# Moving an expert's first transposes and slot rows ahead of the conditional block in a two-layer mixture-of-experts kernel

## The chip, the cores and the metric

One Trainium2 chip; the program uses one core. The metric is the device time of one execution in microseconds (us), as the median of several runs. TensorE's matmul side is called PE below and its weight loads PEld, VectorE is DVE, ScalarE is ACT, GpSimd is POOL, SyncE is SP. A small q behind an engine's name means its instruction sequencer: what the sequencer does by itself (branching, waiting, loading a register) is not counted as busy time of the engine.

## What is computed

A network of three blocks over 256 tokens of width 1024: two layers of attention or convolution, each followed by a mixture of 16 experts, and then one block of a recurrence and a neighbourhood attention. Only the experts matter here:

```python
def hierarchical_moe(hin, w_group, b_group, w_router, b_router, w_gate, w_up, w_down):
    g_prob = softmax(xf @ w_group + b_group)
    g_w, g_idx = top_k(g_prob, 1)                  # one group of four per token
    e_val, e_idx = top_k(e_logits_of_that_group, 2)  # two experts in it
    e_w = softmax(e_val)
    gates = sum(one_hot(g_idx * 4 + e_idx, 16) * (g_w * e_w))
    y = zeros((256, 1024))
    for e in range(16):
        hid = silu(xt @ w_gate[e]) * (xt @ w_up[e])      # 1024 -> 512
        y = y + gates[:, e:e + 1] * (hid @ w_down[e])    # 512 -> 1024
    return y
```

How many tokens choose an expert depends on the data.

## The kernel before

`moe(l, ...)` runs one layer of experts; l is 0 or 1. It ranks the tokens of each expert, and every expert works on a block of 64 slots. If more than 64 tokens chose an expert, further blocks of 64 follow, at most three, each in a nested run-time `If`.

One expert e goes through these steps. `half(e, w, xg, hh)` multiplies the gathered tokens `xg` with the gate and up weights for half hh of the 512 units: `up` writes 32 matmuls into the PSUM tile `gu` (L817, L818), and `hidden` makes `hd` from it with one ACT instruction (`hs`, L828) and one DVE instruction (L829). `turn` transposes `hd` with two PE matmuls into the PSUM tile `hidT` (L836) and copies that to `ht` on DVE (L837). `down` multiplies `ht` with the down weights into `y` (L843). `gated` scales `y` and splits it into two parts `Y` (DVE L850 and L854, ACT L853). `oht_of(e, off)` broadcasts the slot ranks with two small matmuls (`oht` in PSUM, L805) and compares them with the slot numbers on DVE (L807); the result `oht` says which token sits in which slot. `scatter` adds `Y` to the tokens' rows in the four PSUM banks `z` through `oht` (four matmuls, L860).

The loop over e overlaps two experts. At its top stands `more(e, w, nv)`: the `If` over further blocks of expert e (`more_tokens`, in the branch). After it come `turn` for the first half of expert e (whose `hd` was made in the loop's turn before), the load of the next expert's block count `nv` from `xi` (L982, L983), a hint for the next branch, `oht_of`, the second `half` of expert e, `down`, `turn`, `down`, `gated`, then the first `half` of expert e + 1, and at last `scatter` of expert e. So each boundary between two loop turns reads on PE: `z` matmuls, the `If`, `hidT`, `oht`, `gu`.

Every engine meets the `If`. Where it is not entered, an engine jumps to a short block that waits until the engine's own earlier instructions are done and then adds to its semaphore what the skipped instructions would have added ("the bump" below). In the profile it is an EVENT_SEMAPHORE of L920 on the engine's sequencer, and the jump is a COMPARE_BRANCH of L920. An instruction after the `If` that waits for a semaphore value from inside the `If` therefore waits for that engine's bump. Such waits come from shared buffers: the PSUM banks of tags A (`gu`, `gat`) and B (`hidT`, `oht`, `y`, `pq`) have two slots each, and the instructions in the `If` use them too.

PE's order is written out by hand in this loop (`manual_schedule`); DVE and ACT keep the order in which a scheduler puts them. The weights come through a ring of 1 MB buffers that SP fills by DMA as `free(2)` gives them back.

Of the kernel before, what the change touches and what calls it, by code (L numbers as in the profile page):

```python
# [10 lines left out]
F32 = mybir.dt.float32  # L11
F32R = mybir.dt.float32r
# [5 lines left out]
THREE = {mybir.EngineType.PE, mybir.EngineType.DVE, mybir.EngineType.Activation}  # L18
PSUM = bass.MemoryType.PSUM

P = 128
D = 1024
NT = 256
# [149 lines left out]
def model(ctx: ExitStack, tc: tile.TileContext, A, out, stop=None):  # L173
# [472 lines left out]
    def moe(l, wr, lb, pl, late):  # L646
        a2, b2 = mod[f"a2_{l}"], mod[f"b2_{l}"]
        with more_ring, tc.tile_pool(name=f"moe{l}", bufs=1, reuse_waits="tile") as mp, \
# [150 lines left out]
                V.tensor_tensor(gs, pg, par, op=OP.mult)  # L799
                V.tensor_reduce(gc[:, 2 * g:2 * g + 2], gs, axis=AX.X, op=OP.add)  # L800

            def oht_of(e, off):
                p = bank("B", "oht")[:, :256]
                for t in range(2):
                    T.matmul(p[:, t * P:t * P + P], rb[:, t, e:e + 1].to_broadcast([P, P]), identb, start=True, stop=True)  # L805
                o = mw.tile([P, NT], F32R, name="oht")
                V.tensor_scalar(o, p, off, None, op0=OP.is_equal)  # L807
                return o

# [22 lines left out]
            def turn(e, hd, ht, hh):  # L832
                us = slice(64 * (e % 2), 64 * (e % 2) + 64)
                pt = bank("B", "hidT")[:, :128].rearrange("p (c s) -> p c s", c=2)
                for c in range(2):
                    T.transpose(pt[:, c], hd[us, c * P:c * P + P], ident[us, us])  # L836
                V.tensor_copy(ht[:, 2 * hh:2 * hh + 2], pt)  # L837
# [35 lines left out]
            def more_tokens(e, w, b, nv):  # L873
                if b < 3:
                    tc.mark_branch_hint_location(f"more{l}_{e}_{b + 1}", hint=nv > b, engines=[mybir.EngineType.PE])
                us = slice(64 * (e % 2), 64 * (e % 2) + 64)
                oe = mp.tile([P, 2, 2, 64], F32R, name="oe")
                re = mp.tile([P, 2], F32, name="re")
                V.tensor_scalar(re, r[:, :, e], -64.0 * b, None, op0=OP.add)
                for t in range(2):  # L880
                    V.tensor_tensor(oe[:, t], iota64[:, None, :].to_broadcast([P, 2, 64]),
                                    re[:, t:t + 1, None].to_broadcast([P, 2, 64]), op=OP.is_equal)
                off = mp.tile([P, 1], F32, name="off")
                V.tensor_scalar(off, slot, 64.0 * b, None, op0=OP.add)
                xe = mw.tile([P, KD, 64], F32, name="xe", tag="yf", bufs=1)
                for k4 in range(2):
                    pe = bank("A", "gat")
                    for k in range(4 * k4, 4 * k4 + 4):
                        ks, c0 = slice(k * P, k * P + P), P * (k % 4)
                        n = 0  # L890
                        for t in range(2):
                            for src in (th, tl):
                                T.matmul(pe[:, c0:c0 + P], src[:, t, ks], oe[:, t], start=n == 0, stop=n == 3)
                                n += 1
                    for k in range(4 * k4, 4 * k4 + 4):
                        c0 = P * (k % 4)
                        if k % 2:
                            S.activation(xe[:, k], pe[:, c0:c0 + 64], AF.Identity, scale=a2[:, k:k + 1], bias=b2[:, k:k + 1])
                        else:
                            V.tensor_scalar(xe[:, k], pe[:, c0:c0 + 64], a2[:, k:k + 1], b2[:, k:k + 1], op0=OP.mult, op1=OP.add)  # L900
                o = oht_of(e, off)
                pq = bank("B", "pq")[:, :1]
                for t in range(2):
                    T.matmul(pq, oe[:, t].bitcast(F32), gates[:, t, e:e + 1], start=t == 0, stop=t == 1)
                ge1 = mp.tile([P, 1], F32, name="ge1")
                V.tensor_copy(ge1, pq)
                ht = mw.tile([P, 4, 64], F32, name="ht")
                p0 = up(e, w, xe, 0)
                hd0 = hidden(e, p0, ge1[us], "x")
                p1 = up(e, w, xe, 1, lambda: turn(e, hd0, ht, 0))  # L910
                hd1 = hidden(e, p1, ge1[us], "x")
                y = bank("B", "y")
                for cs in halves:
                    down(y, w, ht, 0, cs)
                turn(e, hd1, ht, 1)
                finish(y, w, ht, o)

            def more(e, w, nv):
                def block(b):
                    with tc.If(nv > b - 1, label=f"more{l}_{e}" + (f"_{b}" if b > 1 else "")):  # L920
                        with tc.manual_schedule(engines=THREE):
                            more_tokens(e, w, b, nv)
                        if b < 3:
                            block(b + 1)

                block(1)
# [39 lines left out]
            order.close()  # L966
            Yx = cst.tile([P, 2, 512], F32R, name="Y", tag="x0")
            for e in range(16):
                more(e, w, nv)
                with ExitStack() as part:  # L970
                    if e == 15:
                        if l == 1:
                            fg = x[1]
                            junk2 = mp.tile([P, 512], F32, name="junk2", tag="tl")
                        tail.enter_context(tc.manual_schedule(engines=THREE))
                    else:
                        part.enter_context(tc.manual_schedule(engines={mybir.EngineType.PE}))
                    ht = mw.tile([P, 4, 64], F32, name="ht")
                    turn(e, hd0, ht, 0)
                    if e < 15:  # L980

                        nv = nc.values_load(xi[0:1, e + 1:e + 2], min_val=0, max_val=3)  # L982
                        tc.mark_branch_hint_location(f"more{l}_{e + 1}", hint=nv > 0, engines=[mybir.EngineType.PE])  # L983
                    o = oht_of(e, slot)
                    if e == 15:
                        if l == 1:
                            spread(fg, col("fin"))
                    hd1 = half(e, w, xg, 1)
                    y = bank("B", "y")
                    for cs in halves if e == 15 else (slice(0, 512),):  # L990
                        down(y, w, ht, 0, cs)
                    turn(e, hd1, ht, 1)
                    if e in GA:

                        ks = GA[e]
                        if ks[0] == 0:
                            oh = places(e // 4 + 1)
                            xn = mw.tile([P, KD, 256], F32, name="xg", tag="xg")
                        for k in range(*ks, 2):
                            gather(oh, xn, range(k, k + 2))  # L1000
                    if e == 15:
                        finish(y, w, ht, o)
                        free(2)
                        x[0] = cst.tile([P, D], F32, name="x0")
                        for h in range(2):
                            for t in range(2):
                                cs = slice(h * 512, h * 512 + 512)
                                sq = square(t, h, src=z[t][h])
                                if l == 0:
                                    V.tensor_copy(x[t][:, cs], z[t][h])  # L1010
                                else:

                                    V.tensor_tensor(x[t][:, cs], z[t][h], fg[:, cs], op=OP.mult)
                        if l == 1:
                            for h in range(2):
                                for t in range(2):
                                    cs = slice(h * 512, h * 512 + 512)
                                    if (h, t) in SQD:
                                        V.tensor_tensor_reduce(junk2, x[t][:, cs], x[t][:, cs], 1.0, 0.0, op0=OP.mult, op1=OP.add, accum_out=ssq2[:, t, h:h + 1])
                                    else:  # L1020
                                        sq = square(t, h, ssq2)
                        break
                    down(y, w, ht, 1)
                    free(2)
                    Y = gated(y)[1]
                    w = [take(f"moe{l}", e + 1, t) for t in range(6)]
                    if e % 4 == 3:
                        xg = xn
                        slot_gates(e // 4 + 1, oh)
                    hd0 = half(e + 1, w, xg, 0)  # L1030
                    scatter(o, Y)
# [614 lines left out]
```

## Time and profile before

| what | value |
|---|---|
| median of 3 runs | 1191.7 us (1190.25 to 1200.09) |
| the profiled execution: time, span | 1196.26 us, 1194.4 us |
| PE busy | 1103.3 us, 92% of the span |
| DVE busy | 644.3 us, 54% |
| ACT busy | 415.2 us, 35% |
| granted TensorE clock over the span | 0.983 of full speed |
| experts of layer 0, of layer 1 in the span | about 190 to 425 us, and 594 to 863 us |

The span runs from the first to the last instruction in the trace. Times in rows are from the span's start. In a row of the timeline stand: start, duration, engine, line, operation, output<-inputs, sizes, how many instructions were merged, and in brackets how long the engine had been idle and what released it. In a row of grouped lines the last two parts are the busy time with the mean of one in ns, and the idle time just before these instructions with its releasers.

### The profile page before, as it was taken

How to read it: one execution, taken by the hardware profiler on the slowest of the kernel's cores; microseconds unless marked ns; L12 is line 12 of the kernel's file. 1: busy time of each engine (PE TensorE's matmuls, PEld its weight loads, DVE VectorE, ACT ScalarE, POOL GpSimd, SP SyncE). 2: the span in 40 equal slices, each digit the busy share in tenths (PEclk: the TensorE clock that was granted, in tenths of full speed). 3: DMA queues.
4: the chain of work that ended last, by engine and by line, in shares of the span. 5: the costliest groups of instructions: out<-in, count | busy, mean ns of one | idle time of the engine just before them, and what ended most of it. 6: DMA issues, size and time to landing. Idle time of an engine off the chain costs nothing. (4 is left out here: it accounts for less than half of the span.)

```text
span 1194.4 us, 20819 instructions
## 1 busy us (share of the span) xinstructions
PE 1103.3 (92%) x8172; PEld 787.8 (66%) x8172; DVE 644.3 (54%) x1488; ACT 415.2 (35%) x802; POOL 23.1 (2%) x48
## 2 busy tenths in 40 slices
PE   5899998999999989999998998998889999999996
PEld 3786565555555469867654554554478889788995
DVE  4665564333333359887632333332399897667566
ACT  2434432111111154365311211111257546455443
POOL 0000000000000000000000000000012000000000
PEclk9899989999999999999999999999999999999998
DMA  9999868999999987668857999998466445543440
GB/s 381 406 396 418 333 232 340 416 415 416 418 417 418 396 311 291 241 227 324 343 218 281 406 407 393 381 406 317 170 212 217 156 148 181 177 165 140 146 172 36
DMA packets 51064, 354.42 MB, mean 297 GB/s; under 512 B 6160, under 2 KB 6544, under 8 KB 9296
## 3 DMA queue, kind: packets, MB, share of 16 engines
q1 hardware_dynamic: 48544, 344.59, 73.7%
q0 software_dynamic: 2064, 7.08, 1.9%
q8 instruction: 104, 1.70, 0.6%
q14 instruction: 64, 0.52, 0.1%
q10 hardware_dynamic: 288, 0.52, 0.1%
HBM read 350.07 MB, written 1.05 MB: 294 GB/s over the span
## 5 line engine op out<-in xcount | busy, mean ns | idle before, releaser
L818 PE MATMUL gu<-ring,xg 128*64 128x256 f32 x1024 | 240.6, 389 | 2.3 <-issue 2.3
L817 PE MATMUL gu<-ring,xg 128*64 128x256 f32 x1024 | 240.3, 389 | 1.9 <-issue 1.8
L473 PE MATMUL pw<-xh,wh 128*128 128x256 f32 x736 | 211.5, 289 | 7.5 <-ACT wh L456 2.6
L459 DVE TENSOR_TENSOR wl<-ring,wh 128x1024 fp32r<-128x1024 f32 x144 | 175.2, 1221 | 74.3 <-ACT wh L456 70.2
L475 PE MATMUL pw<-xh,wl 128*128 128x256 f32 x736 | 209.2, 285 | 0.8 <-DVE wl L459 0.8
L474 PE MATMUL pw<-xl,wh 128*128 128x256 f32 x736 | 208.6, 284 | 0.0
L817 PEld LDWEIGHTS gu<-ring,xg 128*64 128x64 f32 x1024 | 139.6, 140 | 70.5 <-issue 11.2
L456 ACT ACTIVATE wh<-ring 128x1024 fp32r<-128x1024 f32 x114 | 120.0, 1058 | 152.4 <-PE pw L474 75.6
L473 PEld LDWEIGHTS pw<-xh,wh 128*128 128x128 f32 x736 | 141.3, 193 | 19.1 <-issue 10.0
L818 PEld LDWEIGHTS gu<-ring,xg 128*64 128x64 f32 x1024 | 139.6, 140 | 18.9 <-issue 10.4
L475 PEld LDWEIGHTS pw<-xh,wl 128*128 128x128 f32 x736 | 141.6, 193 | 3.5 <-DVE wl L459 1.9
L474 PEld LDWEIGHTS pw<-xl,wh 128*128 128x128 f32 x736 | 141.7, 193 | 0.9 <-DVE ge L1084 0.4
L843 PE MATMUL y<-ring,ht 128*64 128x512 f32 (+1 forms) x576 | 128.3, 563 | 6.7 <-DVE ht L837 5.0
L829 DVE SCALAR_TENSOR_TENSOR hd<-hs,gc,gu 64x256 f32<-64x256 f32 x64 | 30.7, 480 | 165.8 <-ACT hs L828 165.8
L828 ACT ACTIVATE hs<-gu 64x256 f32<-64x256 f32 x66 | 25.0, 378 | 252.1 <-PE gu L818 252.1
L353 PE MATMUL ada<-ring,zc 128*32 128x256 f32 x960 | 68.9, 393 | 14.0 <-DMA ring<-ada 11.3
L843 PEld LDWEIGHTS y<-ring,ht 128*64 128x64 f32 x576 | 39.4, 137 | 53.6 <-issue 33.8
L853 ACT ACTIVATE Y<-yf 64x512 fp32r<-64x512 f32 (+1 forms) x72 | 42.7, 593 | 91.3 <-DVE yf L850 90.4
L854 DVE TENSOR_TENSOR Y<-yf,Y 64x512 fp32r<-64x512 f32 (+1 forms) x72 | 46.2, 642 | 22.7 <-ACT Y L853 21.3
L490 PE MATMUL pt<-wh,xh 128*128 128x512 f32 x144 | 57.0, 398 | 1.0 <-ACT wh L456 0.4
L492 PE MATMUL pt<-wl,xh 128*128 128x512 f32 x144 | 56.5, 392 | 0.5 <-DVE wl L459 0.5
L491 PE MATMUL pt<-wh,xl 128*128 128x512 f32 x144 | 56.3, 391 | 0.0
(391 smaller groups left out, 1528.0 us busy)
## 6 DMA issues: line engine op xcount, KB each, us to landing
ring<-moe SPq DMA_DIRECT2D x192, 1024.0 KB, 9.5
ring<-ada SPq DMA_DIRECT2D x60, 1024.0 KB, 9.5
ring<-b_z SPq DMA_DIRECT2D x24, 1024.0 KB, 4.8
ring<-b_x SPq DMA_DIRECT2D x12, 1024.0 KB, 5.5
ring<-od_q SPq DMA_DIRECT2D x8, 1024.0 KB, 10.1
ring<-ev_q SPq DMA_DIRECT2D x6, 1024.0 KB, 18.2
ring<-ev_v SPq DMA_DIRECT2D x4, 1024.0 KB, 15.6
ring<-ev_o SPq DMA_DIRECT2D x4, 1024.0 KB, 15.7
```

Of the source, the lines that this page charges most:

```text
L353: T.matmul(p[32 * j:32 * j + 32, :256], zc[:, k, 7 - r:39 - r], w[:, k], start=start and k < 4, stop=stop and k >= 4, skip_group_check=True)
L456: S.activation(h, w, AF.Copy)
L459: V.tensor_tensor(l, w, h.bitcast(F32), op=OP.subtract)
L473: T.matmul(p, hk, xh[:, k], start=k == 0, stop=False)
L474: T.matmul(p, hk, xl[:, k], start=False, stop=False)
L475: T.matmul(p, lk, xh[:, k], start=False, stop=k == KD - 1)
L490: T.matmul(p[t], xh[:, k, n], hk, start=k == 0, stop=False)
L491: T.matmul(p[t], xl[:, k, n], hk, start=False, stop=False)
L492: T.matmul(p[t], xh[:, k, n], lk, start=False, stop=k == KD - 1)
L817: T.matmul(p[gs_], xg[:, k], wg[:, k], start=k == 0, stop=k == KD - 1)
L818: T.matmul(p[us], xg[:, k], wu[:, k], start=k == 0, stop=k == KD - 1)
L843: T.matmul(y[64 * h:64 * h + 64, cs], ht[:, k], wd[:, k % 2, h, cs], start=k == 0 and cs.start == 0, stop=k == 3, skip_group_check=cs != s ...
```

## The change

`turn(e, hd0, ht, 0)` and `oht_of(e, slot)` now stand ahead of `more(e, w, nv)`, in a block whose order is fixed on PE, DVE and ACT. Inside the `If`, the tiles of the same kind take other memory, so that those made ahead of it stay whole: `ohx` uses the buffer `junk`, and `htx` the buffer `e`.

```diff
-            def oht_of(e, off):
+            def oht_of(e, off, o=None):
                 p = bank("B", "oht")[:, :256]
                 for t in range(2):
                     T.matmul(p[:, t * P:t * P + P], rb[:, t, e:e + 1].to_broadcast([P, P]), identb, start=True, stop=True)
-                o = mw.tile([P, NT], F32R, name="oht")
+                o = mw.tile([P, NT], F32R, name="oht") if o is None else o
                 V.tensor_scalar(o, p, off, None, op0=OP.is_equal)
                 return o
...
-                o = oht_of(e, off)
+                o = oht_of(e, off, wk.tile([P, 512], F32R, name="ohx", tag="junk", bufs=1)[:, :NT])
...
-                ht = mw.tile([P, 4, 64], F32, name="ht")
+                ht = adap.tile([P, 256], F32, name="htx", tag="e").rearrange("p (a b) -> p a b", a=4)
...
             for e in range(16):
+                with tc.manual_schedule(engines=THREE):
+                    ht = mw.tile([P, 4, 64], F32, name="ht")
+                    turn(e, hd0, ht, 0)
+                    o = oht_of(e, slot)
+
                 more(e, w, nv)
...
-                    ht = mw.tile([P, 4, 64], F32, name="ht")
-                    turn(e, hd0, ht, 0)
                     if e < 15:

                         nv = nc.values_load(xi[0:1, e + 1:e + 2], min_val=0, max_val=3)
                         tc.mark_branch_hint_location(f"more{l}_{e + 1}", hint=nv > 0, engines=[mybir.EngineType.PE])
-                    o = oht_of(e, slot)
```

On PE, behind the `If` of expert 1 in layer 0, stood before (the names in brackets are the semaphores that an instruction waits for: DVE_49, PE_49 and Activation_49 count finished instructions of the engines, DMAHW ones landed transfers):

```order
L920 UNCONDITIONAL_BRANCH [waits PE_49] x3
L836 MATMUL hidT<-ident,hd 128x64 [waits DVE_49,PE_49]
L836 MATMUL hidT<-ident,hd 128x64
L982 TENSOR_LOAD xi
L983 REGISTER_ALU
L1634 BRANCH_PREFETCH_HINT
L805 LDWEIGHTS rb [waits DVE_49]
L805 MATMUL oht<-identb,rb 128x128 [waits PE_49]
L805 LDWEIGHTS rb
L805 MATMUL oht<-identb,rb 128x128
L817 MATMUL gu<-ring,xg 64x256 [waits DMAHW3_49,Activation_49]
```

and stands now:

```order
L920 UNCONDITIONAL_BRANCH [waits PE_49] x3
L985 TENSOR_LOAD xi
L986 REGISTER_ALU
L1636 BRANCH_PREFETCH_HINT
L817 MATMUL gu<-ring,xg 64x256 [waits DVE_49,DMAHW3_49,PE_49,Activation_49]
L818 MATMUL gu<-ring,xg 64x256 [waits DMAHW4_49]
```

The wait for DVE_49 has moved from the first `hidT` to the first `gu`. In the built program that `gu` wants a DVE count of 378, while DVE stands at 327 ahead of the `If` and at 387 after its bump; the same holds, with other numbers, behind all 32 of the outermost `If`s (behind the last of layer 1 for the matmuls of L429, which come first there). Ahead of the next `If`, PE now reads:

```order
L860 MATMUL z<-Y,oht 128x512 [waits DVE_49]
L860 MATMUL z<-Y,oht 128x512
L836 MATMUL hidT<-ident,hd 128x64 [waits DVE_49]
L836 MATMUL hidT<-ident,hd 128x64
L805 LDWEIGHTS rb
L805 MATMUL oht<-identb,rb 128x128 [waits PE_49]
L805 LDWEIGHTS rb
L805 MATMUL oht<-identb,rb 128x128
L920 COMPARE_AND_BRANCH
```

Before, the COMPARE_AND_BRANCH stood right behind the `z` matmuls. On DVE, the copy and the comparison now stand ahead of the same `If`, between `hd` and the branch, where before the load of `xi` followed `hd` directly:

```order
L829 SCALAR_TENSOR_TENSOR hd<-hs,gc,gu 64x256 [waits Activation_49]
L837 COPY ht<-hidT 128x128 [waits PE_49]
L807 TENSOR_SCALAR oht<-oht,slot 128x256 [waits PE_49]
L985 TENSOR_LOAD xi
L920 COMPARE_AND_BRANCH
```

DVE's bump waits for both of them. No instruction is added to or taken from PE, DVE, ACT or POOL; on SP one 1 MB transfer of layer 0 stands one `If` earlier.

## Rows read from the trace of the kernel before


**Rows 1.** Windows: busy us and instructions of each engine, PEclk, DMA share, GB/s

```profile
211.00:425.00 214.00, 200.86 (x1436) 113.64 (x1434) 68.69 (x145) 35.41 (x70) 0.00 (x0) 1.00 1.00 410
```

**Rows 2.** Waits of PE: total us, times, longest us

```profile
PE hidT L836 <- DVEq L920: 11.2, 18, 1.8
PE hidT L836 <- PEq L920: 7.5, 14, 1.5
```

**Rows 3.** Lines: busy us, mean ns, then idle ahead and its releasers

```profile
L805 PE MATMUL oht<-identb,rb 128*128 128x128 bf16 x66 | 9.4, 225 | 9.8 <-PE hidT L836 4.9 <-DVE ht L837 4.8
```

**Rows 4.** Timeline at the boundary of expert 1, layer 0

```profile
210.54 1.20 PE L860 MATMUL z<-Y,oht 128*128 128x512 f32 x4
211.13 0.49 DVE L829 SCALAR_TENSOR_TENSOR hd<-hs,gc,gu 64x256 f32<-64x256 f32 x1 [1.07 <-ACT hs L828]
...
212.04 0.31 PE L836 MATMUL hidT<-ident,hd 64*128 64x64 f32 x2 [0.30 <-PEq L920]
...
212.65 0.28 PE L805 MATMUL oht<-identb,rb 128*128 128x128 bf16 x2 [0.31 <-PE hidT L836]
...
212.86 0.43 PE L817 MATMUL gu<-ring,xg 128*64 128x256 f32 x1
...
212.97 0.48 DVE L807 TENSOR_SCALAR oht<-oht,slot 128x256 fp32r<-128x256 f32 x1 [0.30 <-PE oht L805]
```

**Rows 5.** Sequencers there: ns min/median/max, first and last start

```profile
L920 DVEq EVENT_SEMAPHORE  x1: 21/21/21, 211.7 to 211.7; - x1
L920 PEldq EVENT_SEMAPHORE  x1: 51/51/51, 211.8 to 211.8; - x1
```

**Rows 6.** Timeline at the boundary of expert 3, layer 0

```profile
240.67 0.49 DVE L829 SCALAR_TENSOR_TENSOR hd<-hs,gc,gu 64x256 f32<-64x256 f32 x1 [1.07 <-ACT hs L828]
...
241.74 0.31 PE L836 MATMUL hidT<-ident,hd 64*128 64x64 f32 x2 [0.45 <-DVEq L920]
```

**Rows 7.** DVE's sequencer there

```profile
L920 DVEq EVENT_SEMAPHORE  x1: 21/21/21, 241.6 to 241.6; - x1
```

**Rows 8.** Timeline, expert 0, layer 0: transposes with no branch ahead

```profile
202.68 1.89 PE L843 MATMUL y<-ring,ht 128*64 128x512 f32 x8
...
204.50 0.34 PE L836 MATMUL hidT<-ident,hd 64*128 64x64 f32 x2
```

**Rows 9.** Timeline: boundary of expert 15, layer 1, without load and hint

```profile
849.66 0.30 PE L836 MATMUL hidT<-ident,hd 64*128 64x64 f32 x2 [0.30 <-PEq L920]
849.90 0.29 PE L805 MATMUL oht<-identb,rb 128*128 128x128 bf16 x2
850.00 0.29 DVE L837 COPY ht<-hidT 128x128 f32<-128x128 f32 x1 [0.76 <-PE hidT L836]
...
850.33 0.48 DVE L807 TENSOR_SCALAR oht<-oht,slot 128x256 fp32r<-128x256 f32 x1
```

**Rows 10.** Timeline: boundary of expert 0, layer 0

```profile
196.59 0.31 PE L836 MATMUL hidT<-ident,hd 64*128 64x64 f32 x2 [1.84 <-DVEq L920]
...
197.28 0.28 PE L805 MATMUL oht<-identb,rb 128*128 128x128 bf16 x2 [0.38 <-DVE ht L837]
```

**Rows 11.** PE's branch of L920: all, and that of expert 2, layer 0

```profile
L920 PEldq COMPARE_BRANCH  x34: 89/455/3145, 192.1 to 847.7; - x34
...
L920 PEldq COMPARE_BRANCH  x1: 2140/2140/2140, 223.8 to 223.8; - x1
```

**Rows 12.** DMA queue 8 from 223.35 to 223.75: packets, MB, share

```profile
q8 instruction: 1, 0.02, 16.9%
```

**Rows 13.** Timeline at the boundary of expert 9, layer 1

```profile
761.36 0.30 PE L836 MATMUL hidT<-ident,hd 64*128 64x64 f32 x2 [1.55 <-PEq L920]
```

**Rows 14.** Timeline inside expert 7 of layer 1

```profile
729.57 0.43 PE L818 MATMUL gu<-ring,xg 128*64 128x256 f32 x1 [2.26 <-issue]
```

**Rows 15.** Windows around these two, columns as in rows 1

```profile
757.00:765.00 8.00, 6.14 (x50) 3.75 (x48) 2.36 (x5) 0.72 (x2) 0.00 (x0) 1.00 1.00 409
725.00:734.00 9.00, 6.02 (x36) 3.45 (x38) 0.78 (x2) 0.00 (x0) 0.00 (x0) 0.81 1.00 410
```

## Prediction

> **What bounds the kernel now.** I read three views in turn. First the busy time of the engines over the experts of layer 0: PE works for 200.86 of 214 us, DVE for 68.69 and ACT for 35.41, at a granted clock of 1.00 [rows 1]. So PE is the bound there and what can be won or lost is its idle 13 us. DMA's share is 1.00 too, yet among PE's waits none inside the experts names a DMA, so the weights arrive in time, if barely. Next the waits of PE: ahead of `hidT` it idles 11.2 us for DVE's bump (18 times) and 7.5 us for its own (14 times) [rows 2], and ahead of `oht` 9.8 us [rows 3]. Together 28.5 us over the 32 boundaries, nearly all that PE idles in the experts. The two first boundaries of a layer are dearer, 1.84 + 0.38 = 2.22 us [rows 10]; without them (28.5 - 4.4) / 30 = **0.80 us idle at an ordinary boundary**.
>
> Last the timeline of one boundary, with the end of `z` as zero (expert 1: 210.54 + 1.20 = 211.74) [rows 4]. `hd` ended at -0.12. `hidT` starts at +0.30, behind PE's bump (211.8) [rows 5]. `oht` starts only at +0.91, 0.61 behind `hidT`, though in expert 15, which has no load and no hint there, it is 0.24 behind [rows 9, 4]. So the load and the hint hold PE's sequencer about 0.37 us. `gu` starts at +1.12, as `oht` ends. The comparison runs from +1.23 to +1.71: under `gu`, for nothing.
>
> DVE's bump comes in two kinds. In expert 1 it is at 211.7, about 0.1 us after `hd` ended (211.62) [rows 4, 5]. In expert 3 `hd` ended at 241.16 and the bump is at 241.6, 0.44 us later, and `hidT` follows 0.14 us behind it [rows 6, 7]. PE waited for DVE 18 times, two of them at the first boundaries, so 16 of the 30 ordinary ones are of the late kind [rows 2].
>
> **The change, part by part.**
>
> (a) `hidT` and `oht` ahead of the `If`. Nothing is added or removed, so PE's busy time stays. Where no branch stands ahead, `hidT` starts 0.07 us before the modelled end of the matmuls ahead of it (202.68 + 1.89 = 204.57 against 204.50) [rows 8]; `hd` is done by then. So `hidT` at -0.07, `oht` 0.24 later, ended 0.53 after `hidT` started (849.66 to 850.19) [rows 9], which is +0.46. The 0.80 us of idle ahead of these two vanish: -24 us over 30 boundaries, if nothing took their place.
>
> (b) The wait for DVE moves to `gu`. This is what takes its place. `gu` shares its two slots of tag A with the tiles in the `If`, so it waits for a DVE count that only DVE's bump gives. And the bump now stands behind the copy of `ht` and the comparison. In expert 15 the comparison ends 1.15 us after `hidT` starts (849.66 to 850.81) [rows 9], so now at -0.07 + 1.15 = +1.08. The bump follows 0.1 or 0.44 later, PE 0.14 behind it, and two more semaphores at one instruction I price at 0.05 each, what PE's own event took (51 ns) [rows 5]. That gives `gu` at +1.42 (early kind) or +1.76 (late kind).
>
> (c) PE's own way to `gu`. The load and the hint still stand ahead of `gu`, 0.37 us with the instruction behind. Worse, PE's branch was issued before `z` ran and had 1.2 us of `z` as cover; now it is issued behind `oht`, at about +0.2. Its median is 0.455 us [rows 11], so it ends at about +0.65. The jump and the bump behind it were under that cover and have no row on PE; DVE's 0.1 to 0.44 bound them. Then the load, the hint and the waits, some 0.6 us as between `hidT` and `oht`. So PE's own way gives `gu` at +1.4 to +1.7, about the same as DVE's. I take the later of the two: +1.6 in the early kind, +1.76 in the late one.
>
> The mean is (14 x 1.6 + 16 x 1.76) / 30 = +1.69, and PE's idle at a boundary 1.69 - 0.46 = 1.23 us instead of 0.80: **+0.43 x 30 = 13 us**.
>
> (d) The two first boundaries already wait for DVE. There the comparison (0.48 us) [rows 4] comes out from under `gu`: +0.5 each, 1 us. The one boundary that enters the `If` is charged like the others.
>
> (e) What else moves. Behind the waiting `gu` on PE are 32 more matmuls of that half, and behind those ACT's `hs` and DVE's `hd`; they are PE's work or wait for it, so they shift with it. SP's ring transfers are released by PE and shift too; one of layer 0 stands an `If` earlier, and costs nothing, since no boundary waits for a transfer; POOL has no instruction at the boundaries. DVE and ACT are a third busy [rows 1], so the new order costs them nothing but the place of the bump. The buffers `junk` and `e` are touched only in the `If`: 0.
>
> Sum: 13 + 1 = **+14 us**. Against the profiled execution's own 1196.3 us that is 1210; that execution is 4.6 us above the median of the runs, 1191.7, so the median becomes **1206 us**, +1.2%. Its bounds: all boundaries early and PE's way never later than +1.42 gives 30 x (0.96 - 0.80) + 1 = +6 us, 1198; all late gives 30 x (1.30 - 0.80) + 1 = +16, 1208, and 1210 with PE's way 0.07 behind it. So 1198 to 1210 in this case.
>
> **The rivals.**
>
> *PE's branch becomes the bound.* Half of the branches take over 0.455 us, the longest 3.1 us [rows 11]. If that time starts when the branch is issued, the long ones are no longer covered. Take 15 of them at the middle between median and longest, 1.8 us: they end at +2.0 instead of +0.65, and with jump, bump, load and hint (0.75) `gu` starts at +2.75 instead of +1.69. That is 15 x 1.1 = 16 us on top: 1222. Against it: in expert 2 an instruction packet was already moving in the 0.4 us before its 2.14 us branch [rows 12, 11]; if the fetch runs on its own time, a later branch finds it further on and is shorter. The Trainium skill ("Runtime: NRT & Kernel Launch", section Instruction fetch mechanics) says that a taken branch to a target outside the two pages held forces a fetch of that page before execution goes on, which fits branches of 0.09 to 3.1 us and would make the whole of a long one count here; the packet in the row speaks for a fetch that begins earlier.
>
> *PE's own way alone decides, and it is short.* If DVE's bump did not hold `gu` and the branches were short, PE's bump would come 0.1 us after `oht`, and `gu` 0.75 later, at about +1.31: idle 0.85, 30 x 0.05 + 1 = +2.5. Time 1194, no change. Against it stands the count that `gu` wants, which no instruction ahead of the `If` reaches.
>
> *A gain.* If the load, the hint and the bumps all ran while `hidT` and `oht` still worked, PE would only pay the 0.30 us behind its own bump, as expert 15 does now [rows 9], and a little for the waits, 0.5 in all: 30 x (0.50 - 0.80) = -9, 1183. It decides if `gu` starts sooner than +1.26 (0.46 + 0.80). Against it: the comparison alone ends at +1.08, and the load stands behind the bump.
>
> *The clock.* Longer idle could drop it: after an idle time of 2.26 us in expert 7 [rows 14] the stretch of 9 us around it has a mean of 0.81, so part of it ran at 1.2 GHz; after one of 1.55 us [rows 13] the stretch of 8 us kept 1.00, 2.4 GHz [rows 15]. My 1.23 us is on the safe side of both, so I charge nothing; with the long branches of the first rival some would not be.
>
> **How the numbers follow.** My forecast, 1198 to 1210: 0.60. The branch as bound, 1210 to 1222: 0.18. PE's way short, 1192 to 1198: 0.16. The gain: 0.06. A measurement can tell about 1% here, 11.9 us, so slower means above 1203.6. Within my case, two thirds lie above that (0.40), and all of the branch case: slower 0.58. The rest of my case (0.20), the short way and most of the gain lie within 1%: 0.40. Faster by over 1% needs a gain of 12 us, 0.02. The range takes my case, most of the short way and two thirds of the branch case: 1196 to 1218.
>
> **What would show it.** In the profile after: the idle ahead of `hidT` and `oht` gone (28.5 us before); a new idle ahead of `gu` of L817, about 1.2 us at each boundary, some 37 us in all, ended by DVE's bump where the bump is of the late kind; DVE's copy and comparison ahead of its bump, the comparison ending at about +1.1; and the branches on PE, whose median and longest tell the first rival. I am wrong if `gu` starts before +1.26 (then it is no loss), or if the idle ahead of `gu` is ended by PE's bump at over 2 us (then it is the branch).

## The result and the profile after

The changed kernel takes 1216.05 us (median of 4 runs, 1210.12 to 1218.64) against 1193.38 us before (median of 4). The medians lie 22.7 us apart; the ratio is 1.0163, with an interval of 1.013 to 1.0197, which is 19 us. It is slower, by 19 us where I had 14; the range of 1196 to 1218 holds it. A second measurement of the same kernel (below) gave 1.0139 (1.0108 to 1.0169), 17 us. The profiled execution has a span of 1216.7 us against 1194.4.

PE's waits in the profile of after (us in total, times, longest), to be read against [rows 2, 3]:

```profile
PE gu L817 <- DVEq L920: 34.5, 29, 1.5
...
PE gu L817 <- issue: 4.2, 3, 2.6
...
PE gu L818 <- issue: 2.9, 1, 2.9
...
PE gu L817 <- PEq L920: 2.4, 1, 2.4
...
PE row L429 <- DVEq L920: 1.1, 1, 1.1
PE gat L893 <- DVE oe L881: 1.1, 1, 1.1
...
PE hidT L836 <- DVE hd L829: 1.0, 2, 0.5
```

The 28.5 us ahead of `hidT` and `oht` are down to 1.0. In their place stands one new wait: `gu` waits for DVE's bump at 29 boundaries, 34.5 us in all, 1.19 us each.

The boundary of expert 1 in layer 0 of after (timeline, then the sequencers there), against [rows 4, 5]:

```profile
209.82 1.19 PE L860 MATMUL z<-Y,oht 128*128 128x512 f32 x4
...
210.41 0.49 DVE L829 SCALAR_TENSOR_TENSOR hd<-hs,gc,gu 64x256 f32<-64x256 f32 x1 [1.07 <-ACT hs L828]
210.95 0.33 PE L836 MATMUL hidT<-ident,hd 64*128 64x64 f32 x2
211.22 0.28 PE L805 MATMUL oht<-identb,rb 128*128 128x128 bf16 x2
211.32 0.29 DVE L837 COPY ht<-hidT 128x128 f32<-128x128 f32 x1 [0.43 <-PE hidT L836]
...
211.65 0.48 DVE L807 TENSOR_SCALAR oht<-oht,slot 128x256 fp32r<-128x256 f32 x1
212.51 0.40 PE L817 MATMUL gu<-ring,xg 128*64 128x256 f32 x1 [1.01 <-DVEq L920]
```

```profile
L920 PEldq COMPARE_BRANCH  x1: 440/440/440, 211.0 to 211.0; - x1
L920 PEldq EVENT_SEMAPHORE  x1: 51/51/51, 211.5 to 211.5; - x1
L920 DVEq COMPARE_BRANCH  x1: 56/56/56, 212.0 to 212.0; - x1
L920 DVEq EVENT_SEMAPHORE  x1: 21/21/21, 212.2 to 212.2; - x1
```

`z` ends at 211.01. `hidT` starts at -0.06, `oht` ends at +0.49, the comparison ends at +1.12, DVE's bump comes at about +1.2 and `gu` at +1.50. PE's own bump was there at +0.5. PE's branch was issued at about 0.0 (211.0), where I had +0.2. In the boundary of expert 3 the same steps stand, but DVE's bump is of the late kind and `gu` starts at 1.71 behind the end of `z` (240.97):

```profile
242.68 0.40 PE L817 MATMUL gu<-ring,xg 128*64 128x256 f32 x1 [1.22 <-DVEq L920]
```

Where the 22.3 us of the two spans lie, from the waits above, [rows 2, 3] and the page's first part: boundaries 34.5 + 2.4 + 1.0 - 28.5 = 9.4 us; ahead of L429, behind the last `If`, 1.1; ahead of `gat` in the one `If` that is entered 0.6 (0.46 before); gaps inside `gu` that no wait explains 7.1 - 4.1 = 3.0; and PE's busy time 1111.4 - 1103.3 = 8.1, with the same work. Together 22.2. Of the 3.0 us of gaps, 1.3 stand ahead of the first `gu` behind the entered `If`, which the view puts under issue though it is a boundary too.

```profile
PE 1111.4 (91%) x8172; PEld 809.0 (66%) x8172; DVE 643.7 (53%) x1488; ACT 416.5 (34%) x802; POOL 24.0 (2%) x48
```

The busy time grows because TensorE ran longer at its lower clock, 1.2 GHz. Most of that inside the experts lies in one place, the entered `If` of layer 1. There `gat` had to wait for `oe`, which DVE now makes behind the copy and the comparison: 1.09 us of idle instead of 0.46 (after, then before).

```profile
620.67 0.48 DVE L807 TENSOR_SCALAR oht<-oht,slot 128x256 fp32r<-128x256 f32 x1
...
621.28 0.49 DVE L881 TENSOR_TENSOR oe<-iota,re 128x128 fp32r<-128x128 f32 x2
621.62 0.33 PE L893 MATMUL gat<-oe,th 128*128 128x128 f32 x1 [1.09 <-DVE oe L881]
```

```profile
614.22 0.33 PE L893 MATMUL gat<-oe,th 128*128 128x128 f32 x1 [0.46 <-DVE oe L881]
```

These are the windows behind it (from, to, length in us, busy us and instructions of each engine, PEclk, DMA share, GB/s), after first, then before, both some 2.5 us behind the start of `gat`:

```profile
624.00:632.00 8.00, 8.00 (x40) 6.27 (x41) 1.66 (x6) 1.63 (x4) 0.00 (x0) 0.50 0.01 2
```

```profile
617.00:625.00 8.00, 8.00 (x76) 5.65 (x76) 2.26 (x7) 1.69 (x5) 0.00 (x0) 1.00 0.01 4
```

PE is busy throughout in both, but does 40 instructions where before did 76, at a clock of 0.50 instead of 1.00. In all, some 10 us ran at the lower clock there, which costs about 5. An idle time of that length does not do it everywhere: in layer 0 of after `gu` waits 1.0 to 1.3 us at each of these boundaries, and the clock stays at 1.00.

```profile
211.00:425.00 214.00, 194.32 (x1389) 117.42 (x1390) 66.88 (x141) 35.08 (x68) 0.00 (x0) 1.00 0.99 402
```

### The profile page after: what moved, and what is told of

Same layout as the page of the kernel before. It is cut to its first block, busy times and chain, and to the rows that moved or that the text cites. A ratio compares the mean times of both kernels' runs of the same rounds, so it can differ in the third digit from the quotient of the medians.

```text
span 1216.7 us, 20756 instructions
## 1 busy us (share of the span) xinstructions
PE 1111.4 (91%) x8172; PEld 809.0 (66%) x8172; DVE 643.7 (53%) x1488; ACT 416.5 (34%) x802; POOL 24.0 (2%) x48
## 5 line engine op out<-in xcount | busy, mean ns | idle before, releaser
L817 PE MATMUL gu<-ring,xg 128*64 128x256 f32 x1024 | 239.0, 387 | 41.1 <-DVEq L920 34.5
L473 PEld LDWEIGHTS pw<-xh,wh 128*128 128x128 f32 x736 | 141.6, 193 | 19.1 <-issue 10.8
L843 PE MATMUL y<-ring,ht 128*64 128x512 f32 (+1 forms) x544 | 124.9, 575 | 6.4 <-DVE ht L837 4.6
```

The costliest lines, as they stand in the source:

```text
L473: T.matmul(p, hk, xh[:, k], start=k == 0, stop=False)
L817: T.matmul(p[gs_], xg[:, k], wg[:, k], start=k == 0, stop=k == KD - 1)
L843: T.matmul(y[64 * h:64 * h + 64, cs], ht[:, k], wd[:, k % 2, h, cs], start=k == 0 and cs.start == 0, stop=k == 3, skip_group_check=cs != s ...
```

## The experiments

All were timed in five rounds beside the kernel before. The table takes, from each profile: the idle of PE at the boundaries (ahead of `hidT`, `oht` and `gu`, for a bump or for each other; in e1 also the 15.0 us ahead of `gu`), the gaps ahead of `gu` that the view calls issue, and PE's busy time. The ratio is to the kernel before, with its interval.

| kernel | boundaries | gaps in gu | PE busy | ratio |
|---|---|---|---|---|
| before | 28.5 | 4.1 | 1103.3 | 1 |
| after | 37.9 | 7.1 | 1111.4 | 1.0163 (1.013 to 1.0197) |
| a1_after_again | 37.7 | 7.0 | 1105.9 | 1.0139 (1.0108 to 1.0169) |
| e1_only_oht | 50.5 | 0.8 | 1108.1 | 1.0201 (1.0162 to 1.024) |
| e2_only_turn | 42.3 | 4.7 | 1113.8 | 1.0204 (1.0167 to 1.0242) |
| e3_bank_b | 31.4 | 11.0 | 1106.9 | 1.0174 (1.0146 to 1.0203) |
| e4_bank_b_load | 27.6 | 11.1 | 1114.6 | 1.0179 (1.0157 to 1.0201) |
| e5_before_load | 19.1 | 6.0 | 1103.5 | 0.9938 (0.9912 to 0.9965) |
| e6_after_load | 31.3 | 5.6 | 1105.3 | 1.0057 (1.0029 to 1.0085) |
| e7_before_marks | 31.7 | 11.4 | 1112.7 | 1.0109 (1.0067 to 1.0151) |
| e8_bank_b_load_pad | 54.5 | 8.4 | 1125.0 | 1.0434 (1.0395 to 1.0474) |
| e9_load_early | 19.5 | 4.6 | 1101.0 | 0.9913 (0.988 to 0.9946) |

### The changed kernel again (a1_after_again)

> The changed kernel once more, beside before. My sum of the boundaries is +14 us (ratio 1.012); the profile of after shows 22 us more, with fetch gaps inside gu and longer stretches at 1.2 GHz that the sum does not hold. Theory A (bump is all that the change costs, the rest is chance of this execution): ratio 1.010 to 1.014, and the gaps inside gu and the slow stretches lie elsewhere than in the first profile of after. Rival C (the rest belongs to the change too): ratio 1.016 to 1.019, and the slow stretches again behind the entered If and inside layer 1. In both, gu of L817 waits for DVE's bump at 29 boundaries, 33 to 36 us in all.

The ratio, 1.0139, is at the upper end of what Theory A gave, but its other sign fails. The boundaries and the gaps are those of the first profile, in the same experts, and the stretch at 1.2 GHz behind the entered `If` is there again, 7 us long; the rest of PE's busy time is not (1105.9). So about 11 us of boundaries with L429 and `gat`, 3 us of gaps and 3 to 4 us of clock in the `If` came in both profiles, and some 5 us of the first profile's clock did not come again. Neither theory had it whole: the excess over my sum is real, but smaller than 8 us.

### Only the slot rows, only the transposes (e1_only_oht, e2_only_turn)

e1, against before:

```diff
             for e in range(16):
+                with tc.manual_schedule(engines=THREE):
+                    o = oht_of(e, slot)
                 more(e, w, nv)
...
-                    o = oht_of(e, slot)
```

e2, against before:

```diff
             for e in range(16):
+                with tc.manual_schedule(engines=THREE):
+                    ht = mw.tile([P, 4, 64], F32, name="ht")
+                    turn(e, hd0, ht, 0)
                 more(e, w, nv)
...
-                    ht = mw.tile([P, 4, 64], F32, name="ht")
-                    turn(e, hd0, ht, 0)
```

The tiles in the `If` moved as in the change, for the part that moved.

> Before, with only the slot rows (oht and its comparison) ahead of the If; hidT stays behind it. Theory A: oht runs at -0.05 to +0.23, the comparison ends at about +0.75, DVE's bump comes at +0.8 or +1.15, and hidT, which waits for it, at about +0.95 or +1.3; then load and hint, gu at about +1.6 or +1.9. With 0.58 us of PE work in it the idle is 1.0 to 1.3, 30 x 0.35 = +10 us, ratio 1.007 to 1.010. Rival B (PE's branch without its cover costs the time): the branch is issued behind oht as in after, ratio 1.012 or more, equal for e1 and e2.

> Before, with only the transposes and their copy (hidT, ht) ahead of the If; oht and its comparison stay behind it. Theory A: the copy ends at about +0.60, DVE's bump comes at +0.65 or +1.0, and the comparison runs under gu again; PE's own bump at about +0.45, load and hint, oht at about +1.0 to +1.15, gu at +1.3 to +1.4. With 0.58 us of work in it the idle is 0.7 to 0.85, as before: ratio 0.998 to 1.003. Rival B (the branch without its cover): 1.012 or more.

Neither half alone is better than the whole: both are 2.0% slower than before, though the intervals touch those of the whole. Both came out above their ranges. PE's waits in e1, and one boundary (expert 5, layer 0; `z` ended at 276.41):

```profile
PE hidT L836 <- DVEq L920: 32.9, 30, 2.1
PE gu L817 <- issue: 15.0, 32, 1.8
```

```profile
276.25 0.29 PE L805 MATMUL oht<-identb,rb 128*128 128x128 bf16 x2
...
277.65 0.31 PE L836 MATMUL hidT<-ident,hd 64*128 64x64 f32 x2 [1.11 <-DVEq L920]
...
278.37 0.40 PE L817 MATMUL gu<-ring,xg 128*64 128x256 f32 x1 [0.42 <-issue]
```

The comparison is ahead of DVE's bump, `hidT` waits for the bump, and the load and the hint follow `hidT` on PE, another 0.4 us ahead of `gu`. I had the mechanism and the times of `hidT` (+1.24 here, +0.95 where the bump is early; I had +1.3 and +0.95). The idle at a boundary I had too small, 1.0 to 1.3 us where it is 1.24 to 1.6: `oht` starts 0.16 us before `z` ends, so only 0.44 of the 0.58 us of work that I took off lies behind `z`, and `gu` comes some 0.07 us later.

In e2 I expected no change, because the copy ends early. An ordinary boundary idles 1.02 us in the median instead (waits of PE, then DVE and its sequencer at the boundary of expert 3):

```profile
PE oht L805 <- DVEq L920: 29.6, 29, 1.4
```

```profile
240.78 0.29 DVE L837 COPY ht<-hidT 128x128 f32<-128x128 f32 x1 [0.43 <-PE hidT L836]
...
241.76 0.29 PE L805 MATMUL oht<-identb,rb 128*128 128x128 bf16 x2 [1.02 <-DVEq L920]
```

```profile
L984 DVEq TENSOR_LOAD <-xi x1: 305/305/305, 240.8 to 240.8; - x1
...
L920 DVEq COMPARE_BRANCH  x1: 56/56/56, 241.2 to 241.2; - x1
L920 DVEq EVENT_SEMAPHORE  x1: 21/21/21, 241.7 to 241.7; - x1
```

The copy ends at 241.07, the branch is issued at 241.2 and the bump comes at 241.7. So the bump does not follow the end of DVE's last work by a fixed 0.1 or 0.44 us, as I had read it. It follows DVE's branch, by 0.2 or 0.5 us, and the branch stands behind DVE's own load of `xi` (0.3 us), which is issued only once the copy is under way. The copy is too short (0.29 us) to cover that chain. The rival (a PE branch without its cover costs the same in both) names the same size, but at most boundaries its wait is not what the rows show: 30 of 32 and 29 of 32 are ended by DVE's bump. In e2 it has a part all the same. Three boundaries are ended by PE's bump, 11.7 us in all, two of them behind branches of 4.6 and 5.1 us. Of the 25 us by which the profiled e2 is longer than before, DVE's chain explains about 6 (29 boundaries at some 0.2 us), these two branches 9, and PE's busy time 10.

### The load alone moved, in after and in before (e6_after_load, e5_before_load, e9_load_early)

e6, against after:

```diff
                 with tc.manual_schedule(engines=THREE):
+                    if e < 15:
+                        nv1 = nc.values_load(xi[0:1, e + 1:e + 2], min_val=0, max_val=3)
                     ht = mw.tile([P, 4, 64], F32, name="ht")
...
-                        nv = nc.values_load(xi[0:1, e + 1:e + 2], min_val=0, max_val=3)
+                        nv = nv1
```

> After, with only the load of the next block count moved ahead of the If, on PE and on DVE (in front of hidT and of the copy); gu still waits for DVE's bump. Theory A: PE's own way gets shorter by 0.6 us and this gains nothing where the bump is late; if the late kind of the bump comes from DVE's own load standing in front of its branch, all bumps come at about +1.14 and gu at +1.40: 30 x 0.25 = -7 us against after, ratio 1.006 to 1.010; if not, -2 us, ratio as after. Rival B (PE's load and branch set gu): gu at about +0.9, ratio below 1.000.

The boundary of expert 4 in layer 0 of e6 (DVE and PE, then DVE's sequencer):

```profile
258.77 0.48 DVE L807 TENSOR_SCALAR oht<-oht,slot 128x256 fp32r<-128x256 f32 x1
...
259.56 0.40 PE L817 MATMUL gu<-ring,xg 128*64 128x256 f32 x1 [0.83 <-DVEq L920]
```

```profile
L920 DVEq COMPARE_BRANCH  x1: 56/56/56, 258.8 to 258.8; - x1
L920 DVEq EVENT_SEMAPHORE  x1: 21/21/21, 259.3 to 259.3; - x1
```

Without the load DVE's branch is issued as the comparison starts, and its 0.5 us run under the comparison's 0.48: the bump comes as the comparison ends. `gu` still waits for it at 29 boundaries (27.5 us), but 7 us less than in after. The ratio of 1.0057 is what Theory A gave with the load as the cause of the late bump (1.006 to 1.010, just below its lower end), and the time is now within 1% of before. Rival B is out: `gu` did not come at +0.9.

e5, against before, in the loop turn before (e9 has the same two lines ahead of the second `down`; in both, the first value is loaded ahead of the loop):

```diff
...
-                        nv = nc.values_load(xi[0:1, e + 1:e + 2], min_val=0, max_val=3)
+                        nv = nv1
...
+                    if e < 14:
+                        nv1 = nc.values_load(xi[0:1, e + 2:e + 3], min_val=0, max_val=3)
                     scatter(o, Y)
```

> Before, with only the load of the next block count moved: it stands ahead of the z matmuls of the loop turn before. Nothing is ahead of the If that was behind it but this load. If the load and the hint hold oht for 0.37 us, as the boundary of expert 15 without them says, the idle at a boundary falls from 0.80 to about 0.40 us: -12 us, ratio 0.988 to 0.992. If the hint alone or something else holds oht, ratio 0.998 to 1.000.

> As e5_before_load (load of the next block count ahead of the If, all else as before), with the load earlier still, ahead of the second down, so that it is far from the If on every engine. PE's and DVE's order at the boundary is that of e5, so idle of about 0.40 us at a boundary (19 to 20 us in all against 29 before) and a ratio of 0.990 to 0.995. If it comes out at 1.000 or above with the same boundaries, the place of the code decides more than the load.

PE's waits in e9:

```profile
PE hidT L836 <- DVEq L920: 11.7, 19, 1.8
PE hidT L836 <- PEq L920: 7.8, 13, 1.6
```

The 9.8 us ahead of `oht` [rows 3] are gone, those ahead of `hidT` stay. Both kernels are faster than before, e5 by 0.6% (0.3 to 0.9%) and e9 by 0.9% (0.5 to 1.2%). For e9 that is in the range I gave; e5 is just above its own (0.9938 against 0.988 to 0.992), with boundaries that fell by 9.4 us where I had 12, and gaps 1.9 us longer. So of the two waits at a boundary of before, the one that could be had was the one for PE's load, and no work has to move past the `If` for it.

### The wait for DVE taken away (e3_bank_b, e4_bank_b_load)

e3, against after; `up` in the `If` is called with tag B too:

```diff
-                    pe = bank("A", "gat")
+                    pe = bank("B", "gat")
...
+                for _ in range(2):
+                    T.matmul(bank("A", "mark")[:, :P], rb[:, 0, e:e + 1].to_broadcast([P, P]), identb, start=True, stop=True)
                 pq = bank("B", "pq")[:, :1]
```

e4 has the load of e6 as well.

> After, but the tiles gat and gu inside the If take tag B, and two small matmuls without a reader hold tag A there, so that the first gu behind the If waits for PE's bump and not for DVE's. Theory A (DVE's bump holds gu): the idle of gu named DVEq L920 vanishes, PE's own way (its bump at +0.53, then 0.95 for load, hint and waits, as in the one boundary of after where PE's bump was last) puts gu at about +1.48 instead of +1.65 on average, -0.17 x 30 = -5 us against after, so ratio about 1.008 by my sum or 1.012 by the measured after. Rival B (PE's branch and load alone set gu): gu stays at +1.65 and the ratio that of after. A gain below before would speak against both.

> As e3_bank_b, and the load of the next block count stands ahead of the If, in front of hidT, where the z matmuls cover it. Theory A with PE's own way second: without both waits gu comes some 0.35 us behind PE's bump, at about +0.88, idle 0.42 at a boundary instead of 0.80 before and 1.19 after: 30 x (0.42 - 0.80) = -11 us against before, ratio 0.989 to 0.995. Rival B (the branch itself is the bound): gu stays above +1.2, ratio 1.000 or more.

PE's waits in e3, and one ordinary boundary of e4 (expert 5, layer 0; `z` ended at 273.15):

```profile
PE gu L817 <- PEq L922: 30.4, 30, 2.5
...
PE gu L817 <- issue: 5.9, 4, 2.6
...
PE gu L818 <- issue: 5.1, 2, 2.6
```

```profile
274.12 0.40 PE L817 MATMUL gu<-ring,xg 128*64 128x256 f32 x1 [0.49 <-PEq L922]
```

At the boundaries Theory A holds: no `gu` names DVE's bump, and `gu` comes at about +1.4 in e3 and +0.98 in e4, where I had +1.48 and +0.88. An ordinary boundary of e4 idles 0.49 us instead of 0.80 before. In the time nothing of it is left: they are 1.7 and 1.8% slower than before, where I had 0.8 or 1.2% for e3 and a gain for e4. In e4 the boundaries sum to 27.6 us only because one branch takes 6.1 us and another 3.8; the gaps inside `gu` are 7 us longer than before, and PE's busy time 11 us, since more of it ran at 1.2 GHz. Something other than the waits decides here.

### The place of the code (e7_before_marks, e8_bank_b_load_pad)

e7 is before with the two lines of `mark` and nothing else; e8 is e4 with eight of these matmuls instead of two. They stand in the `If`, which is entered once.

> Before, with only the two small matmuls without a reader that e3 and e4 have inside the If; the If is entered once, so they add under 1 us of work and twelve more instructions that every other boundary jumps over. Theory P (place of the code): the gaps of 1.2 to 3 us inside gu that e3 and e4 show in layer 0 (at four places, none in before) come from where the jumped-over code puts PE's instructions in the 16 KB packets; then this kernel has such gaps in layer 0 too, 6 to 10 us in all with the clock's share behind them on top, ratio 1.006 to 1.015, with the idle at the boundaries as before (about 29 us). Theory D (they come from what e3 and e4 do to the waits): no gaps over 1 us in layer 0, ratio 0.998 to 1.002.

> As e4_bank_b_load, with eight of the small matmuls inside the If instead of two, so that the code that is jumped over is longer; nothing that runs at a boundary differs. Theory P (place of the code): the idle at an ordinary boundary stays 0.49 us, but the gaps inside gu and the long branches (4.3 and 6.1 us in e4) fall at other places or vanish, and the ratio moves by more than 0.005 either way from 1.018; with no gaps and no long branches it would be about 0.99. Theory D: the same gaps in the same experts, ratio 1.015 to 1.021.

PE's waits in e7 and all its branches (ns min/median/max), and then the same of e8:

```profile
PE gu L817 <- issue: 8.5, 5, 2.3
...
PE gu L818 <- issue: 2.9, 3, 1.2
```

```profile
L922 PEldq COMPARE_BRANCH  x34: 82/438/5797, 194.3 to 864.7; - x34
```

```profile
PE gu L817 <- PEq L922: 53.5, 31, 6.4
```

```profile
L922 PEldq COMPARE_BRANCH  x34: 89/442/6407, 195.3 to 900.4; - x34
```

Code that is jumped over costs 1.1% in e7, with the boundaries near those of before (31.7 us, of which 4.7 stand behind one branch of 5.8 us) and gaps of 1.6 to 2.3 us at four places in layer 0, where before has none. In e8 the ordinary boundary is still 0.49 us, but five branches take 5.8 to 6.4 us, and the kernel is 4.3% slower. Theory P holds in both: the length of the skipped code sets where PE has to wait for its instructions. After's own gap in expert 10 of layer 1 shows what such a gap is (timeline of PE, then the instruction queue from 795.0 to 796.5):

```profile
797.77 0.58 PE L817 MATMUL gu<-ring,xg 128*64 128x256 f32 x1 [2.60 <-issue]
```

```profile
q8 instruction: 1, 0.02, 4.3%
```

A packet of 16 KB of instructions moves while PE stands in the middle of a row of equal matmuls that wait for nothing. This one begins 2.5 us before the gap ends. The starts of these packets in the twelve traces show the same elsewhere: all 89 of PE's branches at this `If` that take over 1 us end 2.3 to 2.9 us behind the start of the last packet, and 38 of the 41 gaps over 0.6 us that the view calls issue in `gu` end 2.3 to 2.7 us behind one. The other three are the first `gu` behind the entered `If`. The queue does not name the engine that a packet is for, but by these times a long branch and a gap in `gu` are the same thing: PE waits for a packet that set out late. The Trainium skill ("Runtime: NRT & Kernel Launch", section Instruction fetch mechanics) says that the sequencer fetches 16 KiB blocks while it executes and that crossing one is mostly hidden, but that a taken branch out of the held pages stalls. The runs agree with the second half; with the first only partly, since these gaps lie in straight code: in after the two long ones begin about 3 us behind the jump and end 5.6 and 5.9 us behind it.

## Why the prediction was right, and where it was off

**(a) The transposes and slot rows.** Right. `hidT` at -0.06 (I had -0.07), `oht` ends at +0.49 (+0.46), the 28.5 us ahead of them fell to 1.0.

**(b) The wait moves to `gu` and to DVE's bump.** Right, and it is the cause of what the boundaries lost: 34.5 us at 29 boundaries where I had some 37 at 30; the comparison ends at +1.12 (+1.08), `gu` at +1.50 and +1.71 (+1.6 and +1.76). e6 and e3 show it from both sides: a bump earlier by some 0.25 us in the mean gives 7 us at the boundaries, a `gu` that needs no DVE waits for it nowhere. What I had wrong is what the bump hangs on: on DVE's branch behind DVE's load, not on the end of the comparison. For this kernel the two give the same time within 0.1 us; for e2 they do not, which is some 6 us of what I missed there. I also counted the late kind from PE's waits, 16 of 30; by the time from DVE's branch to its bump it is 20 of 30 in before.

**(c) PE's own way.** Its size was right where it could be seen, by two errors that cancel: PE's branch ended at +0.4 (I had +0.65) and its bump came at +0.5, but the way from the bump to `gu` took 0.85 us in e3 (I had 0.6). It gave +1.4 in e3, and in one boundary of after, where a branch of 1.9 us was last, the idle is 2.4 us. Elsewhere DVE's bump is later.

**(d) The first boundaries.** Wrong by sign: 1.5 us ahead of `gu` and 0.5 ahead of `hidT`, 2.0 in all against 2.22 [rows 10], so -0.2 each instead of +0.5. Together with (b) the term of 14 us measured 10.5 (9.4 and the 1.1 ahead of L429), and 11.8 with the 1.3 ahead of `gu` behind the entered `If`.

**The clock.** This is the step that failed. I charged nothing, because an idle time of 1.55 us had kept the clock at 1.00 [rows 13, 15]. At the boundaries that held, at 1.0 to 1.3 us of idle. But the `If` that is entered, which I priced like any other boundary, lost 0.6 us of wait and then ran 7 to 10 us at half the clock, which costs 3 to 5 us. `gat` waits 1.1 to 1.2 us in the eight profiles with the change or a part of it, and in all eight the longest `gat<-oe,th` matmul takes 415 to 421 ns; in before, e5, e7 and e9 it waits 0.5 us and the longest takes 327 to 330 ns. No run changes this wait alone, so that the idle time is the cause is argued from these twelve profiles and not shown; why the same idle time leaves the clock alone at the boundaries stays open. Before and after, each by x16:

```profile
L893 PE MATMUL gat<-oe,th x16: 272/274/328, 614.2 to 617.6; 128*128 128x128 f32 x16
```

```profile
L893 PE MATMUL gat<-oe,th x16: 272/376/415, 621.6 to 626.6; 128*128 128x128 f32 x16
```

**The gaps inside `gu`.** Not in my sum; 3 us, of which 1.3 belong to the boundary behind the entered `If`. The rest is in experts 7 and 10 of layer 1, which have such gaps in both kernels: 2.3 and 1.5 us before, 2.9 and 2.6 after. By e7 and e8 the place of the code decides on these.

**The rivals.** The branch as the bound did not come about in after:

```profile
L920 PEldq COMPARE_BRANCH  x34: 89/433/1943, 196.4 to 869.4; - x34
```

Median and longest are 0.43 and 1.94 us, against 0.455 and 3.1 [rows 11]. Before has 13 branches over 1 us, after has one. Issued later, the branches found their instructions further on, as the packet in [rows 12] let one expect: such a branch ends some 2.5 us behind the packet's start, whenever it is issued. Where the packet itself sets out late it did come about, with branches over 4.5 us: in e8 five times, in e2 twice, in e4 and e7 once each. So 0.18 was not too much for it: which of the two a kernel gets hangs on its code's length. By the Trainium skill's rule on taken branches ("Runtime: NRT & Kernel Launch", Instruction fetch mechanics) a long branch would count in full; e8 agrees (branches of 5.8 to 6.4 us, idle of as much), and so does the one long branch of after (1.9 us, idle of 2.4). The short own way and the gain are out, as `gu` starts behind +1.26 at every ordinary boundary.

So 14 us forecast against 17 to 19 measured: the boundaries gave 10 to 12, and the rest came from the clock and the gaps, which I had at nothing. That the range holds the result is partly luck. 1216 lies above the 1198 to 1210 of my own case; the upper part of the range was there for long branches, and these did not come about.

**What stays open.** Why a jump over code of a given length makes one packet late and not another was not settled; e7 and e8 show only that it does. How after would run with a better place of its code was not tried; since two small matmuls in skipped code cost before 1.1% (e7), that is not a small matter beside the 1.4 to 1.6% of the change. What speaks for the waits as the main cause is the sum of PE's idle time, and e6.

## What to carry to other kernels

Before work is moved ahead of a branch that is rarely taken, look at what the first instruction behind it waits for: if buffers are shared with the branch's body, it may wait for another engine's way around the branch, as `gu` did here for DVE's, and work of that engine moved ahead makes that way longer. A register load in front of a branch or behind it can be the dearest instruction at the place; moving that alone was worth 0.6 to 0.9% here. Where a kernel jumps over long code, compare an edit with a control that only changes the code's length, since that alone cost 1.1% (e7) and 2.5% (e8 against e4) here.

## What the runs showed of the hardware that I had not expected

- On DVE the bump follows the branch by 0.2 or 0.5 us (212.0 to 212.2, 241.2 to 241.7 above), behind its own load of `xi`, 0.3 us; without the load it is covered by a last instruction of 0.48 us (e6), with it a last instruction of 0.29 us does not cover it (e2).
- PE can stand 1 to 3 us in the middle of straight code for an instruction packet, and up to 6.4 us at a branch (e8). In these twelve traces it goes on 2.3 to 2.9 us behind the start of a packet of 16 KB.
- With PE busy all the time, 8 us ran at a clock of 0.50 behind an idle time of 1.09 us, while in before a boundary with 1.55 us of idle kept 1.00 [rows 13, 15], and so did the boundaries of after in layer 0 with 1.0 to 1.3 us each.
